# First norm from rows of x loaded early, a bias table laid out on the host, the last 512 columns as two halves, two w_out products in one accumulator

## The chip, the cores and the metric

The kernel runs on one core of one Trainium2 chip. The metric is the device time of one execution in microseconds (us): the median of three timed runs. The profile is of one further execution. In its rows PE is the matmul engine (TensorE), PEld its weight load, DVE the vector engine, ACT the scalar engine, POOL the GpSimd engine, SP the engine that only issues DMAs; a name with q (SPq) is the instruction queue of that engine.

## What is computed

Three layers on a sequence of 256 tokens of width 1024, in float32. Layer 0 has rotary grouped attention (8 heads), windowed attention with a relative bias and a sink (8 heads) and attention over a memory of 256 rows; layer 1 has neighbourhood attention (16 heads) and the memory; then comes a mixer of dilated attention and a gated convolution, cross-attention to a second memory, and an MLP, with a norm at the end. The parts that the change touches:

```python
def rmsnorm(x, g):
    y = x * lax.rsqrt(jnp.mean(x * x, axis=-1, keepdims=True) + EPS)
    return y * g
...
    # layer 0
    h = rmsnorm(x, norm_gain[0])
    qa, ka, va, qb, kb, vb, qm, gate = split_cols(h @ w_in_even[0], SPLIT_EVEN)
    ya = global_gqa(rope_2d(rmsnorm(qa, q_norm_a[0]), ...), rope_2d(rmsnorm(ka, k_norm_a[0]), ...), va)
    yb = window_gqa(qb, kb, vb, sink_b[0], rel_bias)
    ym = memory_attn(qm, mk, mv)
    y = jnp.concatenate([ya, yb, ym], axis=-1) * jax.nn.silu(gate)
    x = x + y @ w_out_even[0]
...
    # window_gqa, for one block of queries
    bias = rel_bias[t5_bucket(rel)]
    s = where(|rel| <= 128, q @ k.T * scale + bias, -inf)
    m = maximum(max(s), sink)
    p = exp(s - m)
    o = p / (sum(p) + exp(sink - m)) @ v
...
    # MLP and the end
    a = jax.nn.relu(rmsnorm(x, g_mlp) @ w_up)
    x = x + (a * a) @ w_down
    return rmsnorm(x, g_final)
```

## The kernel before

**Arithmetic.** Every float32 product is made of three matmuls on reduced-precision operands: each operand is split into a high and a low part, and high x high, high x low and low x high are summed in PSUM (`mm3`). A weight tile is loaded by SP as `raw` (three buffers), ACT copies it to the high part `wh`, and DVE subtracts to get the low part `wl` (`split`). The tokens lie in two blocks `t` of 128, the width in 8 pieces `k` of 128. `proj_t` gives a product with columns on the partitions and all 256 tokens along the row, `proj_n` one with tokens on the partitions and 512 columns along the row. When `merge` is set (`proj_sum`), a product uses one 512-wide matmul on the two parts of the activations side by side and one 256-wide one for `wl`, and adds the two halves of the bank on ACT and DVE.

**Order.** The program is recorded first (`Plan.record`), with a modelled cost for each instruction and DMA, and then a list scheduler (`Plan.order`) lays out the order of each engine by priority: the place in the program, plus `nc.bias`, plus `SHIFT` by engine and tile (`wl` on DVE at -20: somewhat earlier). The order of each engine is then fixed, and on the chip an engine waits at an instruction until its inputs are there. A DMA that is no weight load normally waits for the last matmul recorded before it; with `nc.ahead` set it does not. `either` leaves to the scheduler whether ACT or DVE takes an instruction. Background steps (softmax of earlier heads, rope) are fed in by `pace` between the projections. All instructions are issued from line 284, so the profile tells them apart by tile names, such as `t_wl<-t_raw,t_wh`.

**Start.** `consts` loads the gains `gT` from POOL's queue and the first two pieces of transposed x (`xT`) from ACT's, and keeps PE busy with 24 matmuls on zeros (`t_warm`). `layer_even` first makes 896 columns of the input projection in a sweep over k, with the unnormed x times the gain (`t_gh`), four `raw` tiles of two pieces each; the norm is applied at the eviction, by rstd per token. The rstd itself comes from `xT`: two squares of 1024 columns on ACT (`t_sq`), three adds on DVE, matmuls with a column of ones that sum over the partitions (`token_rms`), and the power -0.5 on POOL (`t_rstd`). `spread` then makes a diagonal of it and spreads it with a matrix of ones (`t_at<-t_p,t_ones`), and eight DVE products (`t_xs`) and a split make the normed `hT`, which all further projections of the layer use. Rows of x, which the residual adds need, are loaded as one DMA after the constants of the dilated layer. `rope_tables` multiplies cosine and sine by the gains of the q and k norms on POOL (`t_ropetab`).

**Window bias.** `window_bias` loads a table of 32 x 8 biases and a one-hot matrix of 33 x 512; a matmul (`t_at<-t_oh,t_rb`) lays the biases out by distance, ACT takes it out negated, a DMA writes it to device memory (`wb`), and four POOL DMAs read it back per pair of heads, one row shifted for each partition (`wbias`).

**End of layer 0.** `out_proj` adds y @ w_out to x for each of the three parts of y; each call has its own two PSUM banks for each 512 columns and one DVE add per block of tokens.

**MLP.** `up_first` makes the first 512 hidden columns with three 256-wide matmuls per piece; the other seven use `proj_sum`. `down_last` is the last 512 hidden columns of the down projection: for each block of tokens the two halves of 512 columns, then the add to x, the square sum, the product with the final gain (`xg`), rstd, the scaling by rstd and two stores on SP.

## Time and profile before

| | us |
|---|---|
| median of three timed runs | 777.58 |
| lowest, highest | 776.47, 778.34 |
| the profiled execution | 778.79 |
| its span, from its first instruction to its last | 776.7 |

The granted clock of PE was 0.997 of full speed over the profiled execution. A row of the order of time reads: start, length, engine, line, operation, output<-inputs, shapes, count of merged instructions, and in brackets how long the engine was idle before it and what ended that. A row of a group reads: line, engine, operation, names, shapes and count, then busy us, mean ns of one, idle time of the engine before them. Ends of matmuls are modelled and overlap, so the distance between two starts is the cost of a matmul, not its length. A DMA row of a group gives its size and the median us from issue to landing.

### The profile page before, as it was taken

How to read it: one execution, taken by the hardware profiler on the slowest of the kernel's cores; microseconds unless marked ns; L12 is line 12 of the kernel's file. 1: busy time of each engine (PE TensorE's matmuls, PEld its weight loads, DVE VectorE, ACT ScalarE, POOL GpSimd, SP SyncE). 2: the span in 40 equal slices, each digit the busy share in tenths (PEclk: the TensorE clock that was granted, in tenths of full speed). 3: DMA queues.
4: the chain of work that ended last, by engine and by line, in shares of the span. 5: the costliest groups of instructions: out<-in, count | busy, mean ns of one | idle time of the engine just before them, and what ended most of it. 6: DMA issues, size and time to landing. Idle time of an engine off the chain costs nothing.

```text
span 776.7 us, 11891 instructions
## 1 busy us (share of the span) xinstructions
PE 762.4 (98%) x4396; PEld 663.3 (85%) x4396; DVE 615.4 (79%) x1127; ACT 531.0 (68%) x1034; POOL 71.9 (9%) x105
## 2 busy tenths in 40 slices
PE   8999999999999999999999999999999999999996
PEld 7898888888888888888888898899989888888885
DVE  5899988998779789979998889876677655555654
ACT  6687976975679668757786787466556765555562
POOL 0550010000001421132011100100000000000000
PEclk9999999999999999999999999999999999999998
DMA  8993546435557854765348635456535655656541
GB/s 284 314 263 116 163 151 203 163 115 194 181 189 246 240 169 144 208 201 190 115 157 244 190 126 177 132 163 218 189 110 163 186 186 173 206 176 209 168 160 54
DMA packets 109092, 140.47 MB, mean 181 GB/s; under 512 B 3635, under 2 KB 80627, under 8 KB 109036
## 3 DMA queue, kind: packets, MB, share of 16 engines
q1 hardware_dynamic: 103244, 131.33, 52.2%
q0 software_dynamic: 5504, 8.14, 4.7%
q8 instruction: 34, 0.56, 0.3%
q10 hardware_dynamic: 288, 0.26, 0.1%
q14 instruction: 22, 0.18, 0.1%
HBM read 134.98 MB, written 1.06 MB: 175 GB/s over the span
## 4 chain that ended last, share of the span: by engine, by line
PE 85%; ACT 5%; DVE 5%; DMA 2%; issue 2%; POOL 1%; POOLq 0%; SPq 0%; DVEq 0%
PE t_mm L284 63%; PE t_at L284 22%; ACT t_p L284 2%; DVE t_wl L284 1%; ACT t_wh L284 1%; DMA t_raw<-in_w_in_even_dram 1%; DVE t_p L284 1%; DMA t_gq<-in_q_norm_a_dram 1%; POOL t_ropetab L284 1%; ACT t_ph L284 0%; DVE t_y L284 0%; DMA t_xT<-in_x_t_dram 0%; POOL t_rstd L284 0%; ACT t_y L284 0%; DVE t_x L284 0%
## 5 line engine op out<-in xcount | busy, mean ns | idle before, releaser
L284 DVE TENSOR_TENSOR t_wl<-t_raw,t_wh 128x1024 fp32r<-128x1024 f32 (+2 forms) x238 | 288.9, 1217 | 66.7 <-ACT t_wh L284 66.0
L284 ACT ACTIVATE t_wh<-t_raw 128x1024 fp32r<-128x1024 f32 (+2 forms) x238 | 249.9, 1054 | 71.1 <-PE t_mm L284 54.4
L284 PE MATMUL t_mm<-t_mT,t_wh 128*128 128x512 f32 (+1 forms) x512 | 181.3, 394 | 0.0
L284 PE MATMUL t_mm<-t_mT,t_wl 128*128 128x256 f32 x496 | 131.3, 283 | 0.0
L284 PE MATMUL t_mm<-t_wh,t_yh 128*128 128x512 f32 x288 | 113.4, 394 | 0.0
L284 PE MATMUL t_mm<-t_wh,t_yl 128*128 128x512 f32 x288 | 113.2, 394 | 0.2 <-DVE t_yl L284 0.2
L284 PE MATMUL t_mm<-t_wl,t_yh 128*128 128x512 f32 x288 | 112.6, 391 | 0.0
L284 PEld LDWEIGHTS t_mm<-t_mT,t_wh 128*128 128x128 f32 x512 | 93.7, 188 | 13.6
L284 PEld LDWEIGHTS t_mm<-t_mT,t_wl 128*128 128x128 f32 x496 | 93.3, 189 | 6.2
L284 PE MATMUL t_at<-t_mT,t_wh 128*128 128x512 f32 (+1 forms) x256 | 86.6, 382 | 0.0
L284 PE MATMUL t_mm<-t_wh,t_gh 128*128 128x256 f32 (+2 forms) x256 | 64.9, 335 | 0.6 <-ACT t_gh L284 0.6
L284 ACT COPY t_sum<-t_mm 128x256 f32<-128x256 f32 x88 | 32.5, 370 | 46.9 <-PE t_mm L284 46.7
L284 PEld LDWEIGHTS t_mm<-t_wh,t_yl 128*128 128x128 f32 x288 | 54.1, 188 | 11.3 <-DVE t_yl L284 0.6
L284 PEld LDWEIGHTS t_mm<-t_wl,t_yh 128*128 128x128 f32 x288 | 54.1, 188 | 10.9
L284 PE MATMUL t_at<-t_mT,t_wl 128*128 128x256 f32 x240 | 63.1, 281 | 0.0
L284 PEld LDWEIGHTS t_mm<-t_wh,t_yh 128*128 128x128 f32 x288 | 54.1, 188 | 10.3
L284 ACT ACTIVATE t_p<-t_p,t_st 128x256 f32<-128x256 f32 (+1 forms) x113 | 54.0, 493 | 12.3 <-DVE t_st L284 12.2
L284 PEld LDWEIGHTS t_at<-t_mT,t_wh 128*128 128x128 f32 x256 | 46.4, 188 | 7.4 <-issue 0.2
L284 POOL TENSOR_TENSOR t_rstd<-t_rstd,t_mhalf 128x2 f32<-128x2 f32 (+1 forms) x12 | 11.1, 927 | 429.6 <-DVE t_rstd L284 429.6
L284 DVE TENSOR_TENSOR t_sum<-t_mm,t_sum 128x256 f32<-128x256 f32 x88 | 37.2, 422 | 14.8 <-ACT t_sum L284 14.0
L284 PEld LDWEIGHTS t_at<-t_mT,t_wl 128*128 128x128 f32 x240 | 45.2, 189 | 3.7
L284 PE MATMUL t_mm<-t_hT,t_wh 128*128 128x512 f32 (+1 forms) x160 | 48.2, 357 | 0.0
(187 smaller groups left out, 1411.3 us busy)
## 6 DMA issues: line engine op xcount, KB each, us to landing
t_raw<-in_w_in_odd_dram SPq DMA_DIRECT2D x20, 1024.0 KB, 5.2
t_raw<-in_w_up_dram SPq DMA_DIRECT2D x16, 1024.0 KB, 5.5
t_raw<-in_w_down_dram SPq DMA_DIRECT2D x16, 1024.0 KB, 5.0
t_raw<-in_w_in_dram SPq DMA_DIRECT2D x12, 1024.0 KB, 5.3
t_raw<-in_w_in_even_dram SPq DMA_DIRECT2D x10, 1024.0 KB, 6.3
t_raw<-in_w_mem_kv_dram SPq DMA_DIRECT2D x8, 1024.0 KB, 5.0
t_raw<-in_w_out_even_dram SPq DMA_DIRECT2D x6, 1024.0 KB, 5.1
t_raw<-in_w_out_odd_dram SPq DMA_DIRECT2D x6, 1024.0 KB, 5.1
```

What stands on the lines that cost most here:

```text
L284: f(*[self.real(v) for v in args], **{k: self.real(v) for k, v in kwargs.items()})
```

## The change

The gains are loaded from ACT's queue and the first piece of `xT` from SP's. The constants and gains of `rope_tables` are loaded with `ahead`. The rows of x are loaded as two DMAs, ahead of the last two weight rows of the sweep, which are loaded one by one; the squares are summed along the row (`sums`, `rstd`), so the adds, `token_rms` and the squares of `xT` go. The window's bias comes as a table of 8 x 512 from the host; its sign is no longer turned, so the softmax with a sink takes a maximum. One small product of the rope norm moves from POOL to DVE. The first two `out_proj` of layer 0 become one accumulation (`out_proj2`). `up_first` uses the merged form. In `down_last`, for the second block of tokens, the last 512 columns are made as two halves of 256, the second in a bank of its own; the scaling of the last 512 columns is divided between ACT and DVE, and the last store is issued from ACT. `wl` on DVE goes from -20 to -60.

```diff
@@ consts
-        nc.gpsimd.dma_start(self.g, a["gains"])
+        nc.scalar.dma_start(self.g, a["gains"])
...
-        for k in range(2):
-            self.load_x(k, 1, nc.scalar)
+        for k, queue in enumerate((nc.sync, nc.scalar)):
+            self.load_x(k, 1, queue)
@@ rope_tables
+        nc.ahead = True
         nc.sync.dma_start(self.c[:, :C_DIL], a["const"][:, :C_DIL])
...
+        nc.ahead = False
@@ window_bias: removed
@@ softmax
-                                               scalar=-NEG, op0=ALU.add, op1=ALU.min, accum_out=nmax[:, t:t + 1])
+                                               scalar=-NEG if sink is None else NEG, op0=ALU.add,
+                                               op1=ALU.min if sink is None else ALU.max, accum_out=nmax[:, t:t + 1])
             if sink is not None:
-                nc.vector.tensor_scalar(nmax, nmax, sink[1], None, ALU.min)
-            src, sign = p, -1.0
+                nc.vector.tensor_scalar(nmax, nmax, sink, -1.0, ALU.max, ALU.mult)
+            src, sign = p, -1.0 if sink is None else 1.0
@@ out_proj2
+    def out_proj2(self, w, r0, r1, y0, y1):
+        nc = self.nc
+        for c in range(2):
+            cs = slice(c * 512, (c + 1) * 512)
+            po = self.proj_n(self.wide(w, r0, 4, c * 512), 4, 512, lambda l, k: y0[l][:, k, :], stop=False)
+            self.proj_n(self.wide(w, r1, 4, c * 512), 4, 512, lambda l, k: y1[l][:, k, :], banks=po, start=False)
+            for t in range(2):
+                xv = self.x[:, t, cs]
+                nc.vector.tensor_tensor(xv, po[t], xv, ALU.add)
@@ rope
-            nc.gpsimd.tensor_scalar(rs[t][:, :n], ms[:, :n], 1.0 / 64.0, EPS, ALU.mult, ALU.add)
+            nc.vector.tensor_scalar(rs[t][:, :n], ms[:, :n], 1.0 / 64.0, EPS, ALU.mult, ALU.add)
@@ layer_even
-                          ((0, 2, 0, 768), (0, 2, 768, 896)))
+                          ((0, 2, 0, 768), (0, 2, 768, 896)) if k0 < 6 else ((0, 1, 0, 768), (0, 1, 768, 896)))
             if k0 < 6:
                 self.load_x(k0 + 2, 2, nc.sync)
+            else:
+                for t in range(2):
+                    nc.ahead = True
+                    nc.sync.dma_start(self.x[:, t, :], a["x"][0, t * P:(t + 1) * P])
+                    nc.ahead = False
+                columns(k0, ((1, 2, 0, 768), (1, 2, 768, 896)), raw)
...
-        sq = [self.slot([P, 4, S], "sq", F32) for _ in range(2)]
+        ms, squares = self.sums()
         for c in range(2):
-            nc.scalar.activation(sq[c], self.xT[c], AF.Square, scale=1.0 / 32.0)
-        nc.vector.tensor_tensor(sq[0], sq[0], sq[1], ALU.add)
-        r = self.token_rms(sq[0])
+            squares(c)
+        r = self.rstd(ms)
...
-        nc.sync.dma_start(self.x, a["x"][0].rearrange("(t p) d -> p t d", p=P))
...
-        spread_bias()
...
-        qb = [self.q_stack(self.proj_t(w_in, 768 + 256 * i, hT), -0.125) for i in range(2)]
+        qb = [self.q_stack(self.proj_t(w_in, 768 + 256 * i, hT), 0.125) for i in range(2)]
...
+            wb = a["window"]
+            nc.gpsimd.dma_start(w, bass.AP(wb.tensor, wb.offset + 1024 * i, [[1, P], [512, 2], [1, 384]]))
...
         self.flush("a")
-        self.out_proj(w_out, 0, y["a"])
         self.flush("m")
-        self.out_proj(w_out, 1024, y["m"])
+        self.out_proj2(w_out, 0, 1024, y["a"], y["m"])
@@ up_first
-                            self.mm3(po[2 * i + f], wh[:, k, fs], wl[:, k, fs], hT(0, 4 * c + k), hT(1, 4 * c + k),
-                                     c == 0 and k == 0, c == 1 and k == 3)
-            for f in range(4):
-                square(t, f, 1, po[f].unsqueeze(1))
+                            first, last = c == 0 and k == 0, c == 1 and k == 3
+                            nc.tensor.matmul(of, wh[:, k, fs], hT.both(4 * c + k), start=first, stop=False)
+                            nc.tensor.matmul(o[:, 0, :], wl[:, k, fs], hT(0, 4 * c + k), start=False, stop=last)
+            for i in range(2):
+                u = self.work("sum", [P, 2, S], SB)
+                for f in range(2):
+                    nc.scalar.copy(u[:, f, :], po[2 * i + f][:, 1, :])
+                    nc.vector.tensor_tensor(u[:, f, :], po[2 * i + f][:, 0, :], u[:, f, :], ALU.add)
+                square(t, 2 * i, 2, u)
@@ down_last
+                cuts = [(0, 0, 512), (1, 0, 512)] if tt == 0 else [(0, 0, 512), (1, 0, 256), (1, 256, 512)]
+                for i, (c, b0, b1) in enumerate(cuts):
+                    own = b0 > 0
+                    o = self.psum("at", [P, 512])[:, bs] if own else acc[c][tt][:, bs]
+                    nc.bias = 200 if own else 0
...
+                    if not own:
+                        nc.vector.scalar_tensor_tensor(self.x[:, tt, full], acc[c][tt], r2[:, tt:tt + 1],
+                                                       self.x[:, tt, full], ALU.mult, ALU.add)
...
+                    if own:
+                        nc.vector.scalar_tensor_tensor(xv, o, r2[:, tt:tt + 1], xv, ALU.mult, ALU.add)
+                    self.square_sum(xv, ms[:, i:i + 1])
...
+                if tt == 1:
+                    nc.vector.tensor_tensor(r, r, ms[:, 2:3], ALU.add)
                 nc.gpsimd.tensor_tensor(r, r, self.mhalf[:, :1], ALU.pow)
...
+                nc.vector.tensor_scalar(v[0], v[0], r, None, ALU.mult)
+                nc.sync.dma_start(self.out[0, rows, :512], v[0])
+                nc.scalar.activation(v[1][:, :384], v[1][:, :384], AF.Copy, scale=r)
+                nc.vector.tensor_scalar(v[1][:, 384:], v[1][:, 384:], r, None, ALU.mult)
+                (nc.scalar if tt else nc.sync).dma_start(self.out[0, rows, 512:], v[1])
@@ 
-SHIFT = {("tensor", "mm"): 100, ("vector", "wl"): -20}
+SHIFT = {("tensor", "mm"): 100, ("vector", "wl"): -60}
```

More of the change, by code (lines that the diff above doesn't have):

```diff
@@ L1390, in down_last @@
-                    self.square_sum(xv, ms[:, c, 0:1])
-                    nc.vector.tensor_tensor(xg[c][:, tt, :], xv, gb[:, cs], ALU.mult)
+                            self.nc.tensor.matmul(o, xh, wh[:, j, bs], start=own and k0 + j == 0, stop=False)
+                            self.nc.tensor.matmul(o, xh, wl[:, j, bs], start=False, stop=False)
+                            self.nc.tensor.matmul(o, xl, wh[:, j, bs], start=False, stop=k0 + j == 3)
+                    nc.bias = 0
+                    full = slice(512 * c, 512 * c + 512)
```

77 lines of the change are left out of this document (31 added, 46 removed).

## The prediction

> **What bounds the kernel now.** I read the head of the page first, then a table of stretches (busy time of each engine in each), then the order of time inside the stretches where TensorE (PE) is not full.
>
> ```profile
> span 776.7 us, 11891 instructions
> ...
> PE 762.4 (98%) x4396; PEld 663.3 (85%) x4396; DVE 615.4 (79%) x1127; ACT 531.0 (68%) x1034; POOL 71.9 (9%) x105
> ```
>
> PE is busy in 762.4 of 776.7 us, so at most 14.3 us can be won without taking work off PE. The next view says where they lie (columns: stretch, its length, busy us of PE, weight load, DVE, ACT, POOL, then granted clock, DMA share, GB/s).
>
> ```profile
> 0.00:20.00 20.00, 16.87 (x79) 14.19 (x80) 11.44 (x18) 13.33 (x20) 1.28 (x8) 1.00 0.85 277
> 20.00:27.00 7.00, 5.75 (x32) 4.96 (x31) 4.50 (x8) 2.40 (x6) 5.98 (x13) 1.00 0.94 299
> 27.00:45.00 18.00, 17.89 (x137) 17.28 (x136) 17.53 (x40) 14.45 (x27) 6.46 (x9) 1.00 1.03 336
> 45.00:60.00 15.00, 14.32 (x112) 13.08 (x112) 14.87 (x35) 10.92 (x21) 7.88 (x9) 1.00 0.73 214
> 60.00:100.00 40.00, 38.75 (x233) 32.54 (x232) 39.02 (x70) 35.77 (x85) 0.00 (x0) 1.00 0.43 139
> 100.00:180.00 80.00, 80.00 (x483) 70.03 (x482) 73.21 (x167) 62.09 (x143) 2.99 (x4) 1.00 0.48 161
> 764.00:776.70 12.70, 5.54 (x25) 4.26 (x23) 5.53 (x10) 3.62 (x8) 1.10 (x2) 0.83 0.22 83
> ```
>
> PE idles 3.1 us before 20, 1.25 us in 20:27, 0.1 in 27:45, 0.7 in 45:60, 1.25 in 60:100, nothing in 100:180, and 7.2 us after 764. The seven rows hold 13.6 of the 14.3 us. So there are three places: the start, a stretch from 27 to 100 in which DVE is as full as PE (17.53 of 18.00, 14.87 of 15.00 and 39.02 of 40.00), and the tail. Most edits lie in these.
>
> **The first norm.** In order of time, the wait in 20:27:
>
> ```profile
> 20.70 3.90 POOL L284 TENSOR_TENSOR t_ropetab<-t_cst,t_gq 128x64 f32<-128x64 f32 x6 [18.28 <-DMA t_gq<-in_q_norm_a_dram]
> ...
> 24.56 0.72 POOL L284 TENSOR_TENSOR t_rstd<-t_rstd,t_mhalf 128x2 f32<-128x2 f32 x1
> ...
> 25.31 0.69 ACT L284 ACTIVATE t_p<-t_cst,t_rstd 128x128 f32<-128x128 f32 x2 [3.06 <-POOL t_rstd L284]
> 25.76 0.78 PE L284 MATMUL t_at<-t_p,t_ones 128*128 128x128 f32 x4 [1.25 <-ACT t_p L284]
> ...
> 26.99 2.07 DVE L284 SCALAR_TENSOR_TENSOR t_xs<-t_xT,t_gT,t_y 128x256 f32<-128x256 f32 x5 [2.50 <-ACT t_y L284]
> ```
>
> The power that makes the rstd stands on POOL behind six rope-table products, which waited for the gain rows from memory. PE then waits 1.25 us for the diagonal of rstd, and DVE 2.50 us for its spread. The work of the old norm and of the bias expansion, in order of time:
>
> ```profile
> 17.00 1.22 DVE L284 TENSOR_TENSOR t_sq<-t_sq,t_sq 128x1024 f32<-128x1024 f32 x1
> ...
> 19.14 0.69 DVE L284 TENSOR_TENSOR t_p<-t_sq 128x512 f32<-128x512 f32 x1
> ...
> 20.74 0.56 DVE L284 TENSOR_TENSOR t_y<-t_p 128x256 f32<-128x256 f32 x1
> ...
> 21.68 0.50 PE L284 MATMUL t_at<-t_ones,t_y 128*128 128x1 f32 x4
> 22.05 0.48 PE L284 MATMUL t_mm<-t_wh,t_gh 128*128 128x512 f32 x1
> ...
> 22.29 0.15 DVE L284 TENSOR_SCALAR t_rstd<-t_at 128x2 f32<-128x2 f32 x1
> ```
>
> ```profile
> 46.75 1.02 PE L284 MATMUL t_at<-t_oh,t_rb 33*8 33x512 f32 x2
> 47.70 0.51 PE L284 MATMUL t_mm<-t_hT,t_wh 128*128 128x256 f32 x2
> ```
>
> Removed on PE: the four token-sum matmuls, 22.05 - 21.68 = 0.37 us, and the two bias matmuls, 47.70 - 46.75 = 0.95 us. Removed on DVE: 1.22 + 0.69 + 0.56 + 0.15 = 2.62 us. Added are four squares with a sum along the row, each on ACT or DVE as the planner chooses:
>
> ```profile
> L284 ACT ACTIVATE t_p<-t_x 128x512 f32<-128x512 f32 x13 | 8.2, 627 | 7.2 <-DVE t_x L284 7.1
> ...
> L284 DVE CUSTOM_DVE_ANT_0 t_p<-t_x 128x512 f32<-128x512 f32 x7 | 4.8, 683 | 0.0
> ```
>
> With two on each engine, DVE gets 2 x 0.68 = 1.4 us. The rstd sum (about 0.15, as the removed one at 22.29) and four small scalings moved from POOL (4 x 0.15) bring DVE's additions to about 2.1 us. So DVE is relieved of about 0.5 us of work and of the 2.50 us of idle time, 3.0 us in all, and PE of 1.25 + 0.37 + 0.95 = 2.57 us. Both engines are full from 27 to 100, so the end of that stretch moves by the smaller of the two: **2.57 us**. Bounds: 0 (the relief is absorbed by ACT or by the order before 100) and 2.57 + 1.93 of PE's idle time in 45:60 and 60:100, 4.5.
>
> That the wait goes needs the rows of x to be early. Their load moves from 31.8 us to before the last pair of weights, on SP's queue.
>
> ```profile
> t_x<-in_x_dram SPq DMA_DIRECT2D x1, 1024.0 KB, 9.8
> ```
>
> ```profile
> 7.61 0.64 SPq L284 DMA_DIRECT2D t_xT<-in_x_t_dram  x1
> 10.89 4.51 SPq L284 DMA_DIRECT2D t_raw<-in_w_in_even_dram  x3
> ```
>
> The constants and the two gain rows, which were behind the weights issued at 10.89, now go ahead of the last transposed x too. Three issues of about 0.5 us in front put the x rows at 7.61 + 0.64 + 1.5 = 9.8 us at the earliest. By the 9.8 us from issue to landing they are there at 19.6 us. From landing to the diagonal on PE: two rounds of squares (2 x 0.75, the 0.63 to 0.68 above and something for reading the sum), then 0.15, 0.72 and 0.45 us as above (25.76 - 25.31 is the last), about 3.0 us with the gaps: 22.6, against 25.76 before. What is queued behind: the last two weight rows of the sweep stand behind 1 MB, and at the 299 GB/s of 20:27 that is 3.5 us later. They were issued at 10.89, and now in effect at 14.4; should they take 9.8 us as well, they land at 24.2. At 22.05 PE is still at sweep matmuls (t_mm<-t_wh,t_gh), and without the wait it has the projections of the normed x to do besides, so I count nothing, with 1 us of loss as the bound. What is late next, once the wait is gone, is DVE with the weight splits, full from 27 on.
>
> The Trainium skill, page DMA: Bandwidth & Descriptors, section Bandwidth, gives 6.15 us for a DMA of 1 MB. The row above has 9.8 for one of the same size, beside other transfers, so the measurement goes here. As an estimate from that page the rows of x would land at 16.0 us, and the late rival below would have next to no chance.
>
> **The start.**
>
> ```profile
> 5.81 0.35 DVE L284 TENSOR_SCALAR t_gh<-t_xT,t_gT 128x256 fp32r<-128x256 f32 x1 [4.67 <-DMA t_gT<-in_gains_dram]
> ...
> 8.78 0.95 ACT L284 ACTIVATE t_wh<-t_raw 128x896 fp32r<-128x896 f32 x1 [2.05 <-DMA t_raw<-in_w_in_even_dram]
> ```
>
> The gains on ACT's queue can land up to 1.1 us earlier (the wait for them ended the start). But the second weight row lands at 8.78 in any case, and PE's second sweep waits for it, so the time saved is spent there: **0**. Bounds: 1.1 gained; 0.5 lost (one issue in front of the first weights).
>
> **The window bias** otherwise: one ACT eviction, two DMAs and a POOL product go, all beside full engines: 0. **Two w_out products in one accumulator** remove four adds:
>
> ```profile
> L284 DVE TENSOR_TENSOR t_x<-t_mm,t_x 128x512 f32<-128x512 f32 x32 | 21.6, 687 | 1.4 <-PE t_mm L284 1.1
> ```
>
> 4 x 0.687 = 2.7 us of DVE, around 145 to 165. There PE is full (80.00 of 80.00) and DVE is not, so the cover is PE itself: **0**, with 0.7 either way for a changed order (two PSUM banks are held for twice as long).
>
> **wl earlier in DVE's order (-20 to -60).** No row shows its effect; the nearest is the view of waits:
>
> ```profile
> PE t_mm L284 <- DVE t_wl L284: 2.3, 4, 0.9
> ```
>
> All of it won is -2.3; the same lost to other products of DVE is +2.3. I take a third of the gain, **0.7**, as DVE is the partner of PE from 27 to 100.
>
> **First up-projection.** Three 256-wide matmuls become one of 512 and one of 256.
>
> ```profile
> 653.58 2.59 PE t_at L284 x15
> ...
> 744.83 19.29 PE t_mm L284 x85
> ```
>
> The second is 512-wide alone: 0.227 us each. The first is eight of 512 and seven of 256, so 256 takes (2.59 - 8 x 0.227) / 7 = 0.11. Three are 0.33, the new pair 0.34: **0** (bounds 0.5 either way over 32 pairs). Four copies and four adds are new on ACT and DVE, beside PE's other work.
>
> **The tail.** Its rows, in order of time:
>
> ```profile
> 767.08 6.24 SPq L284 DMA_DIRECT2D out_dram<-t_xg  x4
> ...
> 769.15 0.39 PE L284 MATMUL t_mm<-t_wh,t_yl 128*128 128x512 f32 x1
> 769.58 0.75 DVE L284 SCALAR_TENSOR_TENSOR t_x<-t_mm,t_rstd,t_x 128x512 f32<-128x512 f32 x1 [1.14 <-PE t_mm L284]
> ...
> 770.42 0.63 ACT L284 ACTIVATE t_p<-t_x 128x512 f32<-128x512 f32 x1 [1.95 <-DVE t_x L284]
> ...
> 772.00 0.72 ACT L284 ACTIVATE t_xg<-t_xg,t_rstd 128x512 f32<-128x512 f32 x1 [0.86 <-POOL t_rstd L284]
> ```
>
> ```profile
> L284 DVE SCALAR_TENSOR_TENSOR t_y<-t_at,t_gate 128x256 f32<-128x256 f32 x8 | 3.3, 418 | 0.0
> ```
>
> After the last matmul now come 256 columns, not 512. The add from PSUM falls from 0.75 to about 0.48 (0.418 plus the 0.06 by which 0.75 exceeds 0.687): -0.27. The square falls by about 0.2. One more add to the rstd: +0.17. The scaling is split, 384 columns on ACT (0.6 against 0.72) beside 640 on DVE: -0.05. The last store's issue no longer stands behind another on SP (767.08 + 6.24 ends the second of the pair, 0.6 after the 772.72 of ACT): -0.15. PE itself: twelve matmuls of 512 become 24 of 256, 24 x 0.11 to 0.12 - 12 x 0.227 = -0.1 to +0.2; I take +0.2. Sum -0.27 - 0.2 + 0.17 - 0.05 - 0.15 + 0.2 = **-0.3** (bounds -0.9 and +0.3).
>
> **Sum.** -2.57 - 0.7 - 0.3 = -3.57 us. The profiled execution took 778.79 us (span 776.7, 2.1 around it), 1.2 above the median of the three timed runs, 777.58. So 775.2 beside the profiled one, and 774.0 as a median.
>
> **Rivals.**
> *The x rows are late* (slower). PE's order is fixed by a planner that does not know such latencies; the 1.25 us of today are that kind of wait. If the queue lets the x rows out only at 12.6 us, they land at 22.4 by the 9.8 us and the diagonal is there at 25.4; should PE come to the spread matmuls at 19 us, it stalls 6.4 us. The change is then -3.57 + 6.4 = +2.8 us, 780.4. It decides from a stall of about 5.1 us on (3.57 + 1.55). For it: DMA is at 0.85 to 1.03 until 45. Against: the load is out 16 us before the diagonal of today (9.8 against 25.76), and the stall of today had another cause, POOL's rope table.
> *The gain is given back before 100* (no change): ACT, 35.77 of 40.00, sets the end of that stretch. Then only the tail and little of the wl order stay: -0.3 to -0.8, about 777.0.
> *More is won*: DVE's earlier splits also remove PE's idle time from 45 to 100, 1.93 us, and the start gives its 1.1: -6.6, 771.0. For it: DVE is the one that PE waits for there.
>
> **How the numbers follow.** Forecast 0.60 (own range 772.2 to 775.8), x late 0.10, given back 0.13, more 0.17. A measurement here can tell about 0.2% (1.55 us) from no change. Faster 0.77, same 0.13, slower 0.10. The range goes from 770.3 (more won, with the wl bound) to 777.2 (given back), and leaves out the slow rival and the edges of the others.
>
> **What would show it.** Right: in the profile after, the diagonal matmuls t_at<-t_p,t_ones start before 23.5 us with no wait in front of them, POOL's rope table stands ahead of them by microseconds, t_oh is gone, the stretch 60:100 has less PE idle time, and from the last matmul to the last scaling it takes 2.8 us in place of 3.2. Wrong: a wait of PE before t_ones of over 1 us, sweep matmuls that wait for t_raw after 18 us, or idle time of PE after 100, where there is none now.

## The result, and the profile after

The changed kernel takes 773.77 us (median of 5 runs, 773.40 to 774.88), the kernel before 777.58; in runs side by side on one chip the ratio is 0.9947, with a 95% interval of 0.9934 to 0.9960. So the change wins 3.81 us, 0.5%, where the prediction had 3.57 and 774.0. The profiled execution took 773.77 us too. Three executions with a lower granted clock (828.27 us at 0.85, 1069.40 at 0.655, 827.90 at 0.85) are left out of all medians here, and since the last of them is the profiled one of the kernel with the old first up-projection, nothing is read from that profile. The head of its page and the stretches that were shown of the kernel before (columns as there: stretch, its length, busy us of PE, weight load, DVE, ACT, POOL, then granted clock, DMA share, GB/s; the tail's stretch is that of this execution):

```profile
span 771.9 us, 11841 instructions
...
PE 760.7 (99%) x4370; PEld 662.6 (86%) x4370; DVE 614.3 (80%) x1136; ACT 529.0 (69%) x1034; POOL 66.6 (9%) x98
```

```profile
0.00:20.00 20.00, 18.17 (x84) 15.87 (x85) 11.05 (x20) 11.44 (x20) 4.53 (x18) 1.00 0.91 315
20.00:27.00 7.00, 6.44 (x35) 5.49 (x34) 6.40 (x14) 4.78 (x7) 0.82 (x1) 1.00 0.92 281
27.00:45.00 18.00, 16.66 (x131) 15.93 (x130) 16.95 (x41) 14.57 (x29) 3.69 (x6) 1.00 0.95 297
45.00:60.00 15.00, 14.75 (x120) 14.27 (x118) 14.83 (x32) 11.04 (x20) 7.16 (x7) 1.00 0.74 212
60.00:100.00 40.00, 39.64 (x234) 33.18 (x232) 38.71 (x71) 34.79 (x85) 0.00 (x0) 1.00 0.49 158
100.00:180.00 80.00, 79.96 (x479) 69.98 (x480) 72.47 (x167) 62.03 (x142) 2.96 (x4) 1.00 0.49 159
760.00:771.90 11.90, 5.35 (x35) 4.72 (x34) 6.28 (x15) 3.70 (x10) 1.10 (x2) 0.81 0.23 88
```

PE's idle time fell in four stretches (0 to 20: from 3.13 to 1.83 us; 20 to 27: 1.25 to 0.56; 45 to 60: 0.68 to 0.25; 60 to 100: 1.25 to 0.36) and rose in one: 27 to 45, from 0.11 to 1.34. The sum over the first 100 us goes from 6.42 to 4.34, so 2.08 us less.

How far the changed kernel is ahead can be read at single pieces of PE's work (start of the first matmul of each, us from the start of the span, from the timelines; one execution each):

| piece of work | before | after | ahead by |
|---|---|---|---|
| spread of the first rstd (t_p,t_ones) | 25.76 | 21.77 | 3.99 |
| last matmul of the first sweep (t_wh or t_wl, t_gh) | 33.13 | 30.21 | 2.92 |
| first product of layer even's w_out | 139.79 | 137.29 | 2.50 |
| norm at the end of layer even (t_cst,t_xn) | 197.75 | 195.24 | 2.51 |
| norm before the MLP (t_cst,t_x) | 585.23 | 581.43 | 3.80 |
| last matmul | 769.15 | 765.07 | 4.08 |
| end of the span | 776.69 | 771.95 | 4.74 |

So there are three gains (the start, something between 195 and 585 us, the tail), and between the spread and 45 us a part of the lead is lost again. The profiled execution of before was 1.2 us above its kernel's median, so the 5.0 us between the two profiled executions stand for 3.8 in the medians.

The spread, in order of time in the timeline:

```profile
10.50 1.07 SPq L284 DMA_DIRECT2D t_x<-in_x_dram  x2
...
12.47 4.08 POOL L284 TENSOR_TENSOR t_ropetab<-t_cst,t_gq 128x64 f32<-128x64 f32 x12 [11.49 <-DMA t_gq<-in_q_norm_a_dram]
...
20.57 0.82 POOL L284 TENSOR_TENSOR t_rstd<-t_rstd,t_mhalf 128x2 f32<-128x2 f32 x1 [4.03 <-DVE t_rstd L284]
21.43 0.29 DVE L284 TENSOR_SCALAR t_p<-t_cst,t_rstd 128x128 f32<-128x128 f32 x1 [0.60 <-POOL t_rstd L284]
21.77 0.71 PE L284 MATMUL t_at<-t_p,t_ones 128*128 128x128 f32 x4 [0.56 <-DVE t_p L284]
```

The two loads of x's rows are issued at 10.50 and 11.15 us (the prediction had 9.8) and land at 17.57 and 18.87; the rope table is done at 16.55 and POOL then waits 4.03 us for the sum of squares. PE's wait in front of the spread is 0.56 us instead of 1.25. A wait that follows, in the view of waits of 20 to 46 us (total, times, longest) and in the timeline:

```profile
ACT t_wh L284 <- DMA t_raw<-in_w_in_even_dram: 2.0, 2, 1.6
...
PE t_at L284 <- ACT t_wh L284: 0.9, 1, 0.9
```

```profile
27.63 2.01 ACT L284 ACTIVATE t_wh<-t_raw 128x1024 fp32r<-128x1024 f32 x2 [1.59 <-DMA t_raw<-in_w_in_even_dram]
28.74 0.51 PE L284 MATMUL t_at<-t_hT,t_wh 128*128 128x256 f32 x2 [0.92 <-ACT t_wh L284]
```

The first weights of the gate were issued at 18.77 us and were there at 27.55; before, issued at 19.25, they were there at 24.44. PE gets to them earlier than they come, in this execution. In the eight other profiled kernels of the experiments below that leave x's rows and all that is loaded beside them in this place they landed at 25.49 to 27.44 us, and PE waited for `t_wh` there in only two of these eight (0.67 and 0.68 us). An example without the wait, the kernel with the old window bias, where they landed at 25.49:

```profile
27.00:45.00 18.00, 17.55 (x133) 15.90 (x131) 17.80 (x44) 14.28 (x30) 4.83 (x7) 1.00 0.95 300
```

With x's rows late they took 5.0 to 5.2 us from issue to landing (before, and the run with the old norm), with x's rows early 7.1 to 8.8 us. So the early rows do make these weights late. But the wait for them is a matter of the single execution, and it isn't what the change pays: the first product of w_out starts at 137.08 to 137.29 us in the three executions with the wait and at 136.75 to 137.45 in five of the six without.

The tail:

```profile
765.07 0.28 PE L284 MATMUL t_at<-t_wh,t_yl 128*128 128x256 f32 x1
765.39 0.48 DVE L284 SCALAR_TENSOR_TENSOR t_x<-t_at,t_rstd,t_x 128x256 f32<-128x256 f32 x1
765.97 0.42 ACT L284 ACTIVATE t_p<-t_x 128x256 f32<-128x256 f32 x1 [0.40 <-DVE t_rstd L284]
766.51 0.16 DVE L284 TENSOR_TENSOR t_rstd<-t_rstd,t_ms 128x1 f32<-128x1 f32 x1 [0.18 <-ACT t_p L284]
766.75 0.56 POOL L284 TENSOR_TENSOR t_rstd<-t_rstd,t_mhalf 128x1 f32<-128x1 f32 x1 [4.55 <-DVE t_rstd L284]
767.34 0.61 ACT L284 ACTIVATE t_xg<-t_xg,t_rstd 128x384 f32<-128x384 f32 x1 [0.86 <-POOL t_rstd L284]
767.34 0.68 DVE L284 TENSOR_SCALAR t_xg<-t_xg,t_rstd 128x512 f32<-128x512 f32 x2 [0.67 <-POOL t_rstd L284]
768.11 0.35 ACTq L284 DMA_DIRECT2D out_dram<-t_xg  x1
```

From the end of the last matmul (765.35) to the end of the last scaling (768.02) it takes 2.67 us, 3.18 before (769.54 to 772.72). The ends of matmuls are modelled, in both alike.

### The profile page after: what moved, and what is told of

Same layout as the page of the kernel before. It is cut to its first block, busy times and chain, and to the rows that moved or that the text cites. A ratio compares the mean times of both kernels' runs of the same rounds, so it can differ in the third digit from the quotient of the medians.

```text
span 771.9 us, 11841 instructions
## 1 busy us (share of the span) xinstructions
PE 760.7 (99%) x4370; PEld 662.6 (86%) x4370; DVE 614.3 (80%) x1136; ACT 529.0 (69%) x1034; POOL 66.6 (9%) x98
## 4 chain that ended last, share of the span: by engine, by line
PE 82%; ACT 6%; DVE 6%; DMA 3%; issue 2%; SPq 0%; POOLq 0%; POOL 0%; ACTq 0%; DVEq 0%
PE t_mm L284 61%; PE t_at L284 21%; DVE t_wl L284 2%; DMA t_raw<-in_w_in_even_dram 2%; ACT t_p L284 2%; ACT t_wh L284 2%; ACT t_y L284 1%; DVE t_y L284 1%; DVE t_p L284 1%; DMA t_xT<-in_x_t_dram 0%; ACT t_ph L284 0%; SPq L284 0%; ACT t_sum L284 0%; DVE t_pl L284 0%; DVE t_tanh L284 0%
## 5 line engine op out<-in xcount | busy, mean ns | idle before, releaser
L284 PE MATMUL t_mm<-t_mT,t_wh 128*128 128x512 f32 x496 | 179.6, 401 | 0.0
L284 PE MATMUL t_mm<-t_wh,t_yh 128*128 128x512 f32 (+1 forms) x288 | 113.3, 393 | 0.0
L284 PE MATMUL t_mm<-t_wl,t_yh 128*128 128x512 f32 (+1 forms) x288 | 112.3, 390 | 0.0
L284 PE MATMUL t_mm<-t_wh,t_yl 128*128 128x512 f32 (+1 forms) x288 | 111.9, 391 | 0.0
L284 PEld LDWEIGHTS t_mm<-t_mT,t_wh 128*128 128x128 f32 x496 | 91.0, 188 | 13.4
L284 PE MATMUL t_at<-t_mT,t_wh 128*128 128x512 f32 x240 | 86.0, 395 | 0.0
L284 PEld LDWEIGHTS t_at<-t_mT,t_wh 128*128 128x128 f32 x240 | 44.5, 188 | 8.3 <-issue 0.2
L284 PE MATMUL t_mm<-t_gh,t_wh 128*128 128x512 f32 x128 | 47.3, 404 | 0.0
```

The source lines that it names most:

```text
L284: f(*[self.real(v) for v in args], **{k: self.real(v) for k, v in kwargs.items()})
```

## The experiments

Most runs undo one part of the change, so a part that is worth something makes its run slower than the changed kernel's 773.77. Times are medians; the ratio is to the kernel before, run beside it. Places in the trace ("the first product of w_out", 137.29 us in the changed kernel) are of one execution each.

**The old first norm** (sums over the token from the transposed x, by matmuls), x's rows loaded late, as before; the gain rows and constants stay early:

```diff
-        ms, squares = self.sums()
-        for c in range(2):
-            squares(c)
-        r = self.rstd(ms)
+        sq = [self.slot([P, 4, S], "sq", F32) for _ in range(2)]
+        for c in range(2):
+            nc.scalar.activation(sq[c], self.xT[c], AF.Square, scale=1.0 / 32.0)
+        nc.vector.tensor_tensor(sq[0], sq[0], sq[1], ALU.add)
+        r = self.token_rms(sq[0])
...
+        nc.sync.dma_start(self.x, a["x"][0].rearrange("(t p) d -> p t d", p=P))
```

> The changed kernel with the first norm as before: squares of the transposed x, adds on DVE, sums over the partitions on PE, rows of x loaded after the constants of the dilated layer; the rope tables still load early. Theory (the sum of the prediction): without this part the stretch to 100 us loses the 1.25 us wait and the 0.37 us of matmuls again, some 1.6 us over the changed kernel's 773.8, so about 775.4. Rival A: POOL's rope table was the whole cause, and its early load alone removes the wait: the spread matmuls start before 23 us and the time is within 0.4 us of 773.8. Rival B: the 1 MB of x ahead of the weights costs as much as the new norm wins: the time is 773.0 or less, and no wait of ACT for a weight of the projections stands at 27 us.

776.48 us, ratio 0.9980 (0.9971 to 0.9989): 2.7 us slower than with the new norm, 1.1 more than the theory's 1.6. The first product of w_out starts at 139.03, 1.74 later; the rest stands in two steps, 0.3 us around 374 us and 0.4 around 510. Its spread in the timeline:

```profile
12.98 5.62 POOL L284 TENSOR_TENSOR t_ropetab<-t_cst,t_gq 128x32 f32<-128x32 f32 x11
...
22.42 0.14 DVE L284 TENSOR_SCALAR t_rstd<-t_at 128x2 f32<-128x2 f32 x1
22.70 1.95 POOL L284 TENSOR_TENSOR t_rstd<-t_rstd,t_mhalf 128x2 f32<-128x2 f32 x1 [4.10 <-DVE t_rstd L284]
...
25.14 0.78 PE L284 MATMUL t_at<-t_p,t_ones 128*128 128x128 f32 x4 [0.62 <-ACT t_p L284]
```

POOL is free at 18.60 and waits 4.10 us; the spread comes at 25.14 all the same. So an early rope table alone brings the spread forward by 0.6 us only: the old chain of sums is itself not done before 22.42. The power on POOL took 1.95 us here and 0.72 in the kernel before, for a reason that the profile doesn't show; with 0.72 the spread would by estimate have come at 23.9, which isn't before 23 either. The gate's weights land at 24.61 here, with x's rows behind them, and PE has no wait for them.

**Constants and gain rows not ahead**, with the new norm:

```diff
-        nc.ahead = True
         nc.sync.dma_start(self.c[:, :C_DIL], a["const"][:, :C_DIL])
...
-        nc.ahead = False
```

> The changed kernel with the constants and gains of the rope tables loaded without precedence, as before. Theory: POOL's power for the rstd stands behind the rope table again; the spread matmuls start at 25 us or later, with a wait of PE of 1 us or more, and the time is 1.2 us over 773.8, about 775.0. Rival: the rows of x land at 18.9 us and set the start of the norm, not POOL, and DVE is full afterwards anyway: within 0.3 us of 773.8.

777.32 us, ratio 0.9993 (0.9983 to 1.0004): 3.5 us slower (1.2 was expected), which leaves nothing measurable of the whole change. The timeline of 18 to 31 us, and the stretch 27 to 45:

```profile
18.75 0.81 POOL L284 TENSOR_TENSOR t_rstd<-t_rstd,t_mhalf 128x2 f32<-128x2 f32 x1 [17.77 <-DVE t_rstd L284]
25.39 0.62 DVE L284 TENSOR_SCALAR t_p<-t_cst,t_rstd 128x128 f32<-128x128 f32 x2 [1.74 <-DMA t_cst<-in_const_dram]
25.77 0.79 PE L284 MATMUL t_at<-t_p,t_ones 128*128 128x128 f32 x4
30.81 0.62 PE L284 MATMUL t_at<-t_hT,t_wh 128*128 128x256 f32 x3 [2.74 <-ACT t_hT L284]
```

```profile
27.00:45.00 18.00, 14.59 (x107) 14.06 (x106) 16.30 (x37) 10.55 (x22) 8.85 (x16) 0.91 0.96 306
```

The rstd is there at 19.56, with x's rows issued 3.3 us earlier than in the changed kernel, and POOL has not begun its rope table. But the diagonal is made from the identity, a part of the constants, and DVE waits for those until 25.39. So not POOL holds this spread but the load of the constants. The normed activations that follow from the spread are there at 30.8, while PE has used up the sweep (its last matmul starts at 27.73): PE idles 2.74 us, and the granted clock is 0.91 in this stretch. With the run above: early constants alone put the spread at 25.14, the row norm alone at 25.77, neither at 25.76, both at 21.77.

**The old window bias** (expanded on the chip by two matmuls, written to memory and read back):

```diff
-        self.sink = self.base.tile([P, 8], F32, name="sink")
-        nc.sync.dma_start(self.sink, a["sink_b"].to_broadcast([P, 8]))
+        spread_bias = self.window_bias()
...
         g["a"] = self.gate_tile(w_in, 2048, hT, "at")
+        spread_bias()
```

> The changed kernel with the window bias made on the chip as before (one-hot matmul, eviction, store and read back, negated scores). Theory: the two bias matmuls hold PE for 0.95 us in a stretch where PE counts, so about 774.7. Rival: DVE sets the end of that stretch, the matmuls fall into PE's waits for it, and the time stays within 0.3 us of 773.8.

776.24 us, ratio 0.9985 (0.9976 to 0.9994), 2.5 us slower, above both forecasts. But the first product of w_out starts at 137.14, not later than the 137.29 of the changed kernel: the two matmuls cost nothing where they stand. From 92 to 310 us PE does the same matmuls in the same order at the same times within 0.25 us, and then loses 1.5 us in one place in the middle of layer odd. There, in the timelines of POOL and PE, first the changed kernel's:

```profile
254.80 1.16 POOL L284 DMA_DIRECT2D t_ks<-t_ks  x2 [0.35 <-issue]
256.17 1.26 POOL L284 DMA_DIRECT2D t_rpbraw<-in_rpb_c_dram  x2 [0.21 <-issue]
...
310.59 0.39 PE L284 MATMUL t_at<-t_pl,t_vp 128*128 128x256 f32 x1 [0.26 <-DVE t_pl L284]
```

then that with the old bias:

```profile
255.07 1.16 POOL L284 DMA_DIRECT2D t_ks<-t_ks  x2 [0.67 <-DVE t_ks L284]
260.19 1.25 POOL L284 DMA_DIRECT2D t_rpbraw<-in_rpb_c_dram  x2 [3.96 <-issue]
...
312.07 0.39 PE L284 MATMUL t_at<-t_pl,t_vp 128*128 128x256 f32 x1 [1.66 <-DVE t_pl L284]
```

POOL issues the load of layer odd's position bias 4.0 us later, "issue" standing for a wait of which the profile shows no cause. DVE and ACT come to the softmax late, and PE pays at 312. No instruction of the old bias is near. Another 0.8 us is lost in two later places (0.3 around 376 us, 0.4 around 510), where profiles of the changed kernel's order differ as well.

**The old window bias, and the gains' load on POOL's queue again**, to see whether that wait hangs on what was issued on the queue before:

```diff
-        nc.scalar.dma_start(self.g, a["gains"])
+        nc.gpsimd.dma_start(self.g, a["gains"])
```

> The changed kernel with the old window bias, as in the run that undid it alone (776.24), and besides with the gains' load back on POOL's queue, which by itself cost nothing (773.9). Theory (the 2.5 us of the old window bias are an accident of POOL's queue: there the load of layer odd's position bias was issued 4.0 us late behind four copies of t_ks, and PE stalled 1.8 us for t_pl at 310 us; one transfer more on that queue shifts which transfer it is put behind): no stall over 0.6 us at 310 us, total 773.6 to 774.4. Rival (the old bias itself costs it): the stall is there again, total 775.8 to 776.7.

775.10 us (774.20 to 777.76 in 12 runs), ratio 0.9968 (0.9958 to 0.9979), between the two theories' ranges. The wait is gone (the position bias is issued at 256.7, right behind the copies) and so is the stall at 310. So about 1.1 of the 2.5 us (1.5 in the profile) were that accident. The 1.3 us that stay can't all be put down to the old bias. The profile shows 0.6 of them at the first product of w_out (137.88), where the old bias alone showed none (137.14); PE idles 2.98 us before 20 here and 2.05 there, so they came with the gains' load on POOL's queue. That this load costs nothing by itself was taken from a run that moved a load of transposed x too. What the old bias itself costs in the total isn't settled; the traces show nothing of it up to 310 us.

**t_wl moved 20 places ahead again, not 60:**

```diff
-SHIFT = {("tensor", "mm"): 100, ("vector", "wl"): -60}
+SHIFT = {("tensor", "mm"): 100, ("vector", "wl"): -20}
```

> The changed kernel with the low parts of the weights at -20 in DVE's order as before. Theory: a third of PE's direct waits for them comes back, +0.7, about 774.5. Rival A: no effect on the time, within 0.3 us of 773.8. Rival B: the order alone gave the 1.8 us by which the mixer's stretch (from the first transposes of t_xg to the next norm's) is now shorter: then that stretch is 110.9 us again and the time is about 775.6.

775.35 us, ratio 0.9969 (0.9956 to 0.9981): 1.6 us slower, twice what was expected. PE's waits for `t_wl` over the whole span, of the changed kernel and then of this one (total, times, longest):

```profile
PE t_mm L284 <- DVE t_wl L284: 0.9, 2, 0.6
```

```profile
PE t_mm L284 <- DVE t_wl L284: 1.8, 2, 1.2
```

The longest, 1.17 us, stands at 65.5 us (in the kernel before: 0.94 at 67.9), and no profile with 60 places has it. But it is hardly seen at the first product of w_out, 137.32: that lies 0.0 to 0.2 us behind the executions with 60 places and the same order at the end of layer even (137.08 to 137.29). From 101 to 373 us the matmuls of both kernels start within 0.25 us of each other. The stretches behind that, of the changed kernel and then of this one:

```profile
370.00:380.00 10.00, 10.00 (x66) 8.80 (x65) 9.77 (x20) 8.47 (x21) 0.00 (x0) 1.00 0.33 107
380.00:390.00 10.00, 10.00 (x45) 8.03 (x44) 9.22 (x15) 6.90 (x15) 0.00 (x0) 1.00 0.33 107
390.00:402.00 12.00, 12.00 (x75) 10.62 (x74) 11.96 (x25) 11.71 (x24) 1.85 (x2) 1.00 0.55 177
```

```profile
370.00:380.00 10.00, 9.92 (x65) 8.48 (x65) 9.85 (x21) 7.93 (x19) 0.00 (x0) 1.00 0.10 27
380.00:390.00 10.00, 9.80 (x43) 7.78 (x42) 9.90 (x18) 7.12 (x15) 0.00 (x0) 1.00 0.56 189
390.00:402.00 12.00, 11.71 (x71) 10.10 (x70) 10.72 (x24) 10.97 (x24) 2.33 (x2) 1.00 0.53 175
```

```profile
384.88 0.50 PE L284 MATMUL t_mm<-t_wh,t_yl 128*128 128x512 f32 x1 [0.20 <-DVE t_yl L284]
...
398.41 0.77 PE L284 MATMUL t_at<-t_cst,t_xg 128*128 128x128 f32 x5 [0.29 <-DVE t_xg L284]
```

In the end of layer odd PE has no idle time in the changed kernel and 0.57 us with 20 places. Counted by the distances from one start to the next, there are four gaps (373.7, 378.7, 384.3 and 397.7 us), 1.2 us over the usual distance together; the kernel before has the same four. Two of these gaps (0.8 us) are waits for `t_yl` and `t_xg`, the other two stand in front of products of `t_pl`; none is a wait for `t_wl`. With 60 places the planner puts eleven products of the memory's keys ahead of the norm's transposes, and these fill the largest gap. Both signs of rival B came true (the mixer's stretch is 110.97 us, the time 775.35), but the 1.9 us by which the stretch is longer are those eleven products, which now stand behind its first transposes instead of ahead of them; lost time are only the gaps.

**60 places in that stretch alone**, from the last part of layer odd to the mixer's first transposes, 20 elsewhere:

```diff
-        self.nc.vector.tensor_tensor(l, src, h.bitcast(F32), ALU.subtract)
+        bias = self.nc.bias
+        self.nc.bias = bias - 40 * self.early
+        self.nc.vector.tensor_tensor(l, src, h.bitcast(F32), ALU.subtract)
+        self.nc.bias = bias
...
-SHIFT = {("tensor", "mm"): 100, ("vector", "wl"): -60}
+SHIFT = {("tensor", "mm"): 100, ("vector", "wl"): -20}
```

> The changed kernel with the subtraction that makes t_wl moved only 20 places ahead everywhere, as before, but 60 in the stretch from the last part of layer odd to the mixer's first transposes, where PE's order is then that of the changed kernel again. Theory (what the 60 places are worth is the four small stalls of PE between 373 and 398 us, 1.2 us in all, that the kernel with 20 everywhere has and the changed kernel has not): total within 0.4 of the changed kernel's 773.8. Rival (the gain comes from many small waits for t_wl over the whole span): total as with 20 everywhere, 775.2 to 775.5.

774.13 us (774.03 to 774.65), ratio 0.9957 (0.9943 to 0.9970), 0.4 from the changed kernel and 1.2 from 20 everywhere. The theory holds: that stretch carries the gain. This kernel has the 1.16 us wait for `t_wl` at 65.6 us again, and it costs next to nothing (first product of w_out at 137.45).

**More bytes beside the rows of x:**

```diff
+                more = self.slot([P, 4, S], "sq", F32)
                 nc.ahead = True
                 for t in range(2):
                     nc.sync.dma_start(self.x[:, t, :], a["x"][0, t * P:(t + 1) * P])
+                nc.sync.dma_start(more.rearrange("p a b -> p (a b)"), a["x"][0, 0:P])
                 nc.ahead = False
```

> The changed kernel with 512 KB more loaded right behind the rows of x on SP's queue: the first 128 rows of x a second time, into a tile that nothing reads. Theory (the megabyte of x ahead of the gate's weights is what made them land at 27.55 us and PE stall for 0.9 us at 28.7): half as many bytes again ahead of them land them 1.2 to 1.8 us later, the wait of ACT for them grows by as much, the first product of layer even's w_out comes 0.5 to 1.5 us later than 137.3 us, total 774.3 to 775.3. Rival (the late landing comes from the transfers' fixed part or from the order of the queue, not from bytes): the weights land within 0.4 us of 27.55 and the total stays at 773.8. The spread of the norm stays at 21.8 us by both.

775.17 us, ratio 0.9966 (0.9953 to 0.9978), 1.4 us slower; the first product of w_out starts at 138.19, 0.9 later. Both are in the theory's ranges, but not by its way: the gate's weights land at 27.39, inside the 25.49 to 27.55 us that are found without the edit. The delay sits on the loads behind them; ACT's wait for weights comes 6 us later, in its timeline:

```profile
33.61 1.06 ACT L284 ACTIVATE t_wh<-t_raw 128x1024 fp32r<-128x1024 f32 x1 [1.61 <-DMA t_raw<-in_w_in_even_dram]
```

These weights were also issued later (28.52, against 23.82 of the changed kernel for its second load of the gate), since the planner had put DVE's split of the last sweep row behind the products of the norm (it ends at 28.45 instead of 23.80) and so a buffer came free later. Half a megabyte more, with the order that came with it, costs 1.4 us; the run doesn't show what the bytes alone cost, nor what sets the 27.55.

**The rows of x behind the last two weight rows:**

```diff
+                columns(k0, ((1, 2, 0, 768), (1, 2, 768, 896)), raw)
                 for t in range(2):
                     nc.ahead = True
                     nc.sync.dma_start(self.x[:, t, :], a["x"][0, t * P:(t + 1) * P])
                     nc.ahead = False
-                columns(k0, ((1, 2, 0, 768), (1, 2, 768, 896)), raw)
```

> The changed kernel with the two loads of x's rows issued behind the last two weight rows of the first sweep instead of ahead of them; the order of every other engine is the same. Theory (the bytes ahead of the gate's weights are the same, only the norm gets its rows later): rows of x land about 1 us later, the spread of the norm moves from 21.8 to 22.5 to 23.0 us, the last sweep matmul and the landing of the gate's weights stay within 0.5 us, total 773.8 within 0.6. Rival (the prediction's bound: weight rows behind x hold up the sweep by up to 1 us): the sweep ends earlier and the total falls to 772.8.

773.81 us. The edit did nothing: SP issues x's rows at 10.78 and 11.46, still ahead of these weight rows, since the planner moves them to the front from either place. The question stays open, but the run is a repetition of the changed kernel, and 0.04 us off: every engine's order is the same. Its profiled execution took 777.64 us; from 20 to 508 us PE follows the changed kernel's within 0.3 us, and it loses 3.8 there:

```profile
511.05 2.61 PE L284 MATMUL t_at<-t_cst,t_xn 128*128 128x128 f32 x14 [2.03 <-ACT t_xn L284]
```

ACT had waited 3.5 us for a load of the cross attention's weights. PE's wait is 2.0 us of the loss; then the granted clock was half from 511.8 to 515.2 us (0.50 over 513 to 515), and the matmuls took twice their time. So two profiles of one order of instructions can differ by some 4 us, and a place that a single profile shows is to be read with that in mind.

**The old tail** (the last 512 columns in one piece):

```diff
-                cuts = [(0, 0, 512), (1, 0, 512)] if tt == 0 else [(0, 0, 512), (1, 0, 256), (1, 256, 512)]
-                for i, (c, b0, b1) in enumerate(cuts):
+                for c in range(2):
+                    o = acc[c][tt]
...
```

> The changed kernel with the end of the MLP as before: both halves of 512 columns whole, scaling and stores as before. Theory: +0.3, about 774.1, and from the start of the last matmul to the end of the span 7.5 us as before. Rival: the profile of the changed kernel has 6.9 us there, so +0.7, about 774.5, less the 0.17 us that 24 short matmuls cost PE over 12 long ones.

774.07 us, ratio 0.9955 (0.9942 to 0.9967): 0.3 us slower in the median, with runs of 773.60 to 775.51 against 773.40 to 774.88, so not clear of noise. In the profiles the way from the start of the last matmul to the end of the span is 7.46 us with the old tail, 6.88 with the new.

**The old w_out products, the old first up-projection, the old queues at the start**, each by itself:

```diff
-        self.out_proj2(w_out, 0, 1024, y["a"], y["m"])
+        self.out_proj(w_out, 0, y["a"])
+        self.flush("m")
+        self.out_proj(w_out, 1024, y["m"])
```

> The changed kernel with two separate output products and four more adds on DVE (2.7 us). Theory: PE is full there and DVE is not, so 0: within 0.3 us of 773.8, and the stretch from the first output product to the next norm's transposes stays at 58.0 us. Rival: DVE's adds are late for PE: that stretch grows by 0.5 us or more.

```diff
-                            nc.tensor.matmul(of, wh[:, k, fs], hT.both(4 * c + k), start=first, stop=False)
-                            nc.tensor.matmul(o[:, 0, :], wl[:, k, fs], hT(0, 4 * c + k), start=False, stop=last)
+                            self.mm3(po[2 * i + f], wh[:, k, fs], wl[:, k, fs], hT(0, 4 * c + k), hT(1, 4 * c + k),
+                                     c == 0 and k == 0, c == 1 and k == 3)
...
```

> The changed kernel with the first up-projection as before, three matmuls of 256 columns for each piece. Theory: three of 256 cost PE what one of 512 and one of 256 cost, so 0: within 0.3 us of 773.8, and the stretch from the last transposes of t_x to the last matmul is 173.1 us plus or minus 0.2. Rival: that stretch, 0.5 us shorter in the changed kernel than before, owes it to this edit: 173.5 us and a time of about 774.3.

```diff
-        nc.scalar.dma_start(self.g, a["gains"])
+        nc.gpsimd.dma_start(self.g, a["gains"])
...
-        for k, queue in enumerate((nc.sync, nc.scalar)):
-            self.load_x(k, 1, queue)
+        for k in range(2):
+            self.load_x(k, 1, nc.scalar)
```

> The changed kernel with the gains on POOL's queue and both first pieces of transposed x on ACT's. Theory: 0, as PE's third sweep waits for its weights in any case: within 0.3 us of 773.8. Rival: the first matmul of the sweep comes later by up to 1.1 us and PE never makes it up: about 774.9.

773.50 (ratio 0.9947), 774.17 (0.9959) and 773.38 us (0.9947): none can be told from the changed kernel. With the old w_out products the stretch from the first of them to the next norm's transposes is 57.94 us, 57.95 in the changed kernel, as the theory said. The start is of interest. Its queues do make PE's first 12 us fuller; the stretch 6 to 12 of the kernel with the old queues and then of the changed kernel:

```profile
6.00:12.00 6.00, 5.19 (x24) 3.82 (x24) 4.06 (x8) 3.33 (x6) 0.00 (x0) 1.00 0.95 311
```

```profile
6.00:12.00 6.00, 6.00 (x29) 4.79 (x27) 3.45 (x6) 3.83 (x6) 0.00 (x0) 1.00 0.93 324
```

0.81 us are won there, of which PE's idle time from 12 to 20 takes 0.54 back (0.64 us against 0.10). The spread starts 0.5 us earlier (21.77 against 22.30), yet the first product of w_out starts at 137.29 against 137.16: all of it is given back before.

## Why the prediction was right, and where not

**The first norm and the bias matmuls, -2.57.** At the first product of w_out the kernel is 2.50 us ahead, so the sum holds; its make-up doesn't, and that the two agree so closely is luck. The spread came earlier than predicted (21.77 against 22.6) since x's rows, as two loads of half a megabyte, took 7.1 and 7.7 us from issue to landing and not 9.8; from their landing to the spread it took 2.9 us, 3.0 predicted. That the relief of DVE and PE moves the end of the stretch "by the smaller of the two" was argued, not shown. What the runs show: with the old norm alone 1.74 of the 2.50 are gone; with the old bias alone none; with the start's old queues or 20 places for t_wl none either. The other 0.76 us belong to no single edit.

**The cause named for the wait.** The prediction put it to POOL's rope table behind the gain rows. That is what the trace of before showed last, but taking it away alone moves the spread by 0.6 us (by estimate 1.9, had the power not taken 1.95 us; the old sums end at 22.42). Nor is it the only thing that the early issue does: the identity comes with the constants, and without them the row norm waits at the same 25.8 us. The step held because the change does both.

**The bias matmuls, 0.95 of the 2.57.** Mis-sized: 0 at the first product of w_out. The prediction priced PE's 0.95 us in a stretch in which DVE is as full as PE; that DVE's pace covered them is the likely reading, but no run shows it. That undoing the bias costs 2.5 us in the total is another matter: 1.1 of it came from a late issue on POOL's queue some 200 us on, which no view of before could show, and the rest isn't settled.

**The two weight rows behind x, nothing with 1 us as the bound.** Right for the sweep: its last two rows landed by 21.32 us (24.2 was predicted at the worst), and PE waited for none of them. The delay fell on a load further back: the gate's weights landed 1.0 to 3.1 us later than before (25.49 to 27.55 against 24.44), and in three of nine executions PE waited 0.67 to 0.92 us for them. The prediction had asked who waits for the loads behind x on SP's queue, and stopped at the second of them. At the first product of w_out nothing of these waits is left, so 0 was the right price.

**The start, 0.** The number was right, the reason only in part. The prediction let the second weight row land at 8.78 us in any case and hold PE there; it landed at 6.55, and PE has no idle time from 6 to 12 us (1.49 before). The gains landed 2.6 us earlier (3.17 against 5.78) and not "up to 1.1", a figure for which the prediction shows no row. The time is spent further on: 0.54 of 0.81 us by 20 us, the rest by 137.

**t_wl at 60 places, -0.7.** Sign right, size too small (1.6 us), mechanism wrong. It was estimated as a third of PE's waits for `t_wl`, with DVE as PE's partner from 27 to 100 us. Those waits did fall, from 2.3 to 0.9 us, and the longest is gone, but little of that is seen at 137 us. The gain lies in gaps before products of `t_pl`, `t_yl` and `t_xg` at the end of layer odd, the largest of which the new order fills with products of the memory's keys; one execution of the changed kernel's order shows none of these gaps, others lose 0.3 us around 374.

**Two w_out products in one accumulator, and the first up-projection, 0 each.** Right, within the noise of 0.3 to 0.4 us.

**The tail, -0.3.** In the medians 0.3, not clear of noise. From the end of the last matmul to the last scaling 2.67 us against a predicted 2.8 (0.48 for the add, 0.42 for the square, 0.16 for the extra sum, all as priced).

**The total.** 773.77 against 774.0, the closest part of the account, and in part by luck: the 0.95 us of the bias matmuls that weren't there and the wl order's 0.9 us too few stand against each other.

**The signs named in advance.** t_p,t_ones before 23.5: yes, 21.77. With no wait: no, 0.56 us. Rope table ahead by microseconds: yes, by 4.0. Stretch 60 to 100 with less idle time: yes, 0.36 against 1.25, but this sign belongs to the order of `t_wl`, since with the new norm and 20 places it is 1.39, and with the old norm and 60 places 0.09. Sweep matmuls that wait for `t_raw` after 18 us: none. PE idle after 100: next to nothing, 0.04 in 100 to 180.

**The rivals.** *The x rows are late*: did not happen, but a run shows what such a load can do: with the constants late PE idles 2.74 us and the gain is gone. *Given back before 100* happened in part: of 4.0 us at the spread 2.5 are left. *More is won*: PE's idle time from 45 to 100 fell by 1.32 of the 1.93 us, while 27 to 45 lost 1.23. The total won isn't more for it. The low end of the range, 770.3, doesn't follow from this rival's 771.0 with the bound of the wl order, which would give 769.4; nothing hangs on it here.

The costs of undoing single parts (norm 2.7, bias 2.5, wl order 1.6, up-projection 0.4, tail 0.3, w_out products -0.3, start -0.4; the constants' 3.5 belong with the norm) add up to 6.8 us, nearly twice the 3.8 of the whole. Some of them contain an accident, as that of the bias does, and the last four are within the noise; where the rest of the excess lies isn't shown. They are no shares of the gain.

## What to carry to other kernels

Where a wait has one releaser in the trace, look for what would release it next before calling it the cause; here the row norm and the early constants alone moved the spread by 0 and 0.6 us, and together by 4.0. A load moved ahead can be paid for by loads further behind it than the next; here the gate's weights, behind the two loads that follow it, came 1.0 to 3.1 us later. A wait in one profile isn't yet a cost: this load's was there in three executions of nine and not to be seen 110 us later. PE's 0.95 us of work in a stretch where DVE was as full counted for nothing here, and undoing one edit moved a DMA issue far away, so a part's price needs its place in the trace as well as its median.

## What was not expected of the hardware

- POOL's queue held the issue of a load for 3.96 us with no releaser in the profile (260.19, with the old bias), and not at all with one more transfer at the kernel's start.
- After PE had idled for 2.74 us (constants late) the granted clock was half for 3.4 us, from 31.5 to 34.9, which gives the 0.91 over 27 to 45 us; after 2.03 us of idle time (x's rows "behind") it was half from 511.8 to 515.2. After waits of up to 1.66 us (old window bias, at 312 us) no profile here shows such a drop.
- POOL's power on two columns took 0.72, 0.81, 0.82 and, with the old norm and early constants, 1.95 us; spans on POOL are rough.
- One order of instructions (the changed kernel's and that with x's rows "behind") took 773.09 to 777.64 us, with a late weight load in the profiled execution of 777.64.
